# Turned query and key rows of a hybrid decoder layer: rounding and rest over 128 partitions, stored to DRAM by two transfers

## The chip, the cores and the metric

The kernel runs on one core of one Trainium2 chip. The metric is the time of one execution on the device in microseconds (us). A time taken with a profile comes with its span, from the first to the last instruction of the program on the core, and with the clock that the throttle granted to TensorE, as a share of full speed.

## The reference

One decoder layer over 1024 tokens of width 1024, in float32. One RMS norm and one input projection feed two head groups: differential attention (4 heads) and a gated delta rule (4 heads). Their outputs go through one output projection into the residual stream, and a squared-ReLU MLP of hidden width 4096 follows. What matters here is the differential attention:

```
da_q = rms_norm(da_q.reshape(B, S, DA_HEADS, 2, DA_QK_DIM), q_norm_w[l])
da_k = rms_norm(da_k.reshape(B, S, DA_HEADS, 2, DA_QK_DIM), k_norm_w[l])
...
s = jnp.einsum('bqhcd,bkhcd->bhcqk', qb, k, preferred_element_type=jnp.float32) * scale
...
a = p[:, :, 0] - lam * p[:, :, 1]
return jnp.einsum('bhqk,bkhe->bqhe', a.astype(v.dtype), v)
```

Each head has two softmax maps (index c) of 64 query and key channels each, so the channels of both maps fill 128 partitions.

## The kernel before

**Precision.** TensorE multiplies operands of a rounded type (fp32r in the profile). To keep float32 accuracy each operand is split into its rounded value and its rest (the value minus the rounded value), and products are summed over these parts. For the scores a matmul has room for 128 rows and a map has 64 channels, so for each map the rounded half and the rest are stacked in the partitions of one operand. With the query stacked the same way in `qa` and the other way round in `qb`, two matmuls against the stacked key `KS` (L1148, L1149) give all four products.

**Stages.** The first quarter of the span normalizes the input and computes the gated group's projections. Then comes a stage, from about 258 to 640 us, in which TensorE works through many streams at once: the scan of the gated group (`scan`, `scan_out`), the attention's input projections (`da_units`, `leave`), the turning of its queries and keys (`da_turns`), scores, values, the mixing transposes and the output projection. The rest of the span is the MLP.

**What sets the order.** In the middle stage a planner written into the kernel (`Interleave`) keeps an estimated TensorE time, `flow.now`, and estimated queues of the other engines. Each stream is a generator with a priority; it yields the time from which it can go on. `flow.chain` books instructions on the estimated queues and returns when their result should be there, with 180 ns for each change of engine and a margin of a quarter; `flow.hold` keeps a PSUM bank until then; `flow.put_off` puts a transfer's issue off until its estimated time. The order that comes out is fixed for TensorE. The other engines' orders come from the framework's scheduler. Transfers are issued on SP's queue, one after another, and an issue whose data is not there yet holds back what is behind it on that queue.

**Turning.** `leave` (L1028) takes a projection's PSUM bank `ps_qk` to SBUF on ScalarE (L1040) and normalizes it. `da_turns` (L957) then does 32 steps, one for each block of 128 tokens, for query or key, and for two pairs of heads: two transposes (L965, L966) put the 128 channels of two heads in the partitions of a PSUM tile, 256 columns (two heads of 128 tokens). For each map m, ScalarE rounds the map's 64 partitions into `qa[a, m, :]` (L972), and VectorE writes the rest, value minus rounded, to the other 64 partitions, `qa[b, m, :]` (L973). So a tile takes four instructions over 64 partitions, and `qa` holds each map's operand as it is used later. One transfer stores it (L977) to `qk_d`, where a partition's two maps and two heads lie in one run of 2 KB. `qa` has two buffers.

**Loading.** `load_head` (L1064) reads a head's keys of each map, rows of 512 bytes, and `load_q` (L1081) a block's queries: `qa` in one transfer, `qb` in two with the halves of the partitions exchanged. `load_unit` (L199) brings weights by the transfers of L211 into `wraw`, which ScalarE rounds (L213) and VectorE or GpSimd subtracts (L214). `scan` loads `pka` (L839), `scan_out` loads `pkb` and `zgt` (L894, L896) ahead of their use.

Of the kernel before, what the change touches and what calls it, by code (L numbers as in the profile page):

```python
# [9 lines left out]
F32 = mybir.dt.float32  # L10
F32R = mybir.dt.float32r
BF16 = mybir.dt.bfloat16
AF = mybir.ActivationFunctionType
ALU = mybir.AluOpType
# [4 lines left out]
P = 128  # L19
# [3 lines left out]
NT = SEQ // P  # L23
# [96 lines left out]
def act(n, accum=False):  # L120
    return "S", 55.0 + 0.83 * n + (93.0 if accum else 0.0)


def vec(n, extra=0.0):
    return "V", 68.0 + 1.045 * n + extra
# [7 lines left out]
def tile_hymba_layer(  # L133
# [6 lines left out]
    nc = tc.nc  # L140
    V, S, G, T = nc.vector, nc.scalar, nc.gpsimd, nc.tensor
# [9 lines left out]
    dram = ctx.enter_context(tc.tile_pool(name="dram", bufs=1, space=DRAM))  # L151
# [36 lines left out]
    fsg_d = dram.tile([P, 1024], F32, name="fsg_d")  # L188
    rt_d = dram.tile([SEQ], F32, name="rt_d")
    cgr_d = dram.tile([HEADS * SEQ], F32, name="cgr_d")  # L190
    qk_d = dram.tile([2, 2, NT, P, 2, 2, P], F32, name="qk_d")
    v_d = dram.tile([NT, P, 3, P], F32, name="v_d")
    acc_d = dram.tile([NT, P, DM], F32, name="acc_d")
    ud = {i: dram.tile([FF // 512, P, 2, 512], F32, name=f"ud{i}") for i in range(1, 8)}
# [261 lines left out]
    for tb in range(NT):  # L456
        T.matmul(tail[:, 300 + 2 * tb:302 + 2 * tb], ssum_[:, tb * P:(tb + 1) * P], ones[:, 0:2],
                 start=True, stop=True)
# [305 lines left out]
    flow = Interleave()  # L764
# [3 lines left out]
    HF = (slice(0, 64), slice(64, 128))  # L768
# [185 lines left out]

    late, accs, vts, v_at, qa_free = [], {}, {}, {}, [0.0] * 3

    def da_turns():  # L957
        for i in range(4 * NT):
            while not late:
                yield flow.now + 50, None  # L960
            g, kind, tb, qn, t = late[0]
            r = yield from flow.bank("px", at=max(t + 2000, qa_free[i % 2] - 500))
            late.pop(0)
            pt = px.tile([P, 512], F32, tag="px", name="ps_qkt")
            T.transpose(pt[:, 0:P], qn[:, 0:P], ident)  # L965
            T.transpose(pt[:, P:2 * P], qn[:, P:2 * P], ident)  # L966
            flow.begun(("qa", i % 2))
            qa = sd.tile([P, 2, 256], F32R, tag="qa", name="qa", bufs=2)
            wv = qw if kind == 0 else kw
            for m in range(2):  # L970
                a, b = HF[m], HF[1 - m]
                S.activation(qa[a, m, :], pt[a, 0:256], AF.Copy, scale=wv[a])  # L972
                V.scalar_tensor_tensor(qa[b, m, :], pt[a, 0:256], wv[a], qa[a, m, :].bitcast(F32),  # L973
                                       ALU.mult, ALU.subtract)
            flow.pe(2 * TR)
            t = flow.chain(act(256), act(256), vec(256, 60), vec(256, 60), start=max(flow.now, qa_free[i % 2]))
            flow.put_off(t, ("qa", i % 2), lambda g=g, kind=kind, tb=tb, qa=qa: nc.sync.dma_start(  # L977
                qk_d[g, kind, tb], qa.bitcast(F32).rearrange("p m (h t) -> p m h t", h=2)))
            qa_free[i % 2] = t + DMA_T
            flow.hold(r, t)  # L980
            state["turned"] += 1
            if state["turned"] % (2 * NT) == 0:
                flow.due(lambda t, key: key[0] == "qa")
                state["da"] += 1
                state["da_t"] = flow.now + 6000
        sdctx.close()
# [77 lines left out]
    def load_head(h, pool):  # L1064
        KS = []
        for m in range(2):
            k = pool.tile([P, SEQ], F32R, tag=f"KS{m}", name=f"KS{m}")
            nc.sync.dma_start(k.bitcast(F32).rearrange("p (b t) -> p b t", t=P),
                              qk_d[h // 2, 1, :, :, m, h % 2, :].rearrange("b p t -> p b t"))
            KS.append(k)  # L1070
        return KS

# [8 lines left out]
    def load_q(h, tb):  # L1081
        qa = ap.tile([P, 2, P], F32R, tag="qa", name="qa", bufs=2)
        qb = ap.tile([P, 2, P], F32R, tag="qb", name="qb", bufs=2)
        src = qk_d[h // 2, 0, tb, :, :, h % 2, :]
        nc.sync.dma_start(qa.bitcast(F32), src)
        nc.sync.dma_start(qb[HF[0]].bitcast(F32), src[HF[1]])
        nc.sync.dma_start(qb[HF[1]].bitcast(F32), src[HF[0]])
        return qa, qb
# [5 lines left out]
    def scores():  # L1094
        heads, loaded, npe, nsc, since = {}, {}, 0, 0, 0
        while state["da"] < 1:
            yield flow.now + 300, None
        heads[0] = load_head(0, ap), load_v(0, ap)
        q = load_q(*order[0])
        yield state["da_t"] + 3000, None  # L1100
        for u, (h, tb) in enumerate(order):
            if h == 1 and h not in heads:
                while not (state["scan"] and len(v_at) == NT):
                    yield flow.now + 300, None
                heads[1] = load_head(1, pools["a2"]), load_v(1, pools["a2"])
                loaded[1] = flow.now + 9000
            if h > 0 and state["da"] > 1 and 2 not in heads:
                heads[2] = load_head(2, ap), load_v(2, ap)
                loaded[2] = max(flow.now, state["da_t"]) + 4000
# [8 lines left out]
            if q is None and h > 0:  # L1118
                q = load_q(h, tb)
# [3 lines left out]
            if q is None:  # L1123
                q = load_q(h, tb)
                yield flow.now + 3000, None
# [381 lines left out]
    flow.add(2, values())  # L1507
    flow.add(3, scores())
    flow.add(1.6, da_turns())
    flow.add(4, da_units())  # L1510
    flow.add(1.4, mix_loads())
# [343 lines left out]
```

## Time and profile before

| | |
|---|---|
| median of 3 runs | 1226.64 us (1225.75 to 1227.22) |
| the profiled execution's own time | 1226.58 us |
| its span | 1224.9 us, at a mean granted clock of 0.998 |
| busy VectorE, ScalarE, GpSimd | 850.0, 604.6, 121.0 us |
| instructions of TensorE (matmuls) | 6330 |
| transfers `qk_d<-qa` | 32 of 256 KB, median 3.1 us from issue to landing |

The profiled execution's time is 1.7 us over its span; that part lies outside the program's instructions. It is 0.06 us under the median, so that sums made against it stand for the median too. A busy TensorE is not TensorE at its peak, since the ends of matmuls are modelled; what tells is whether it stood idle and what ended the wait. In the views by stretch, "DMA share" is the mean busy share of the core's 16 DMA engines.

### The profile page before, as it was taken

What the parts mean: (1) busy time and instruction counts of PE and PEld (TensorE: products, weight loads), DVE (VectorE), ACT (ScalarE), POOL (GpSimd) and SP (SyncE); (2) the same over time, 40 slices, a digit from 0 to 9 for tenths busy, and PEclk for the clock granted to TensorE, in tenths of its full rate; (3) what the DMA queues carried; (4) which work ended last, traced back from release to release, by engine and by line L of the source; (5) the groups of instructions that cost most, each with busy time, mean ns of one, the idle gap of its engine ahead of it and who ended that gap; (6) DMA issues with size and microseconds to landing.
All of it is one profiled execution on the core that took longest, in us unless ns stands there. A gap on an engine that the chain in (4) does not pass through costs nothing.

```text
span 1224.9 us, 17632 instructions
## 1 busy us (share of the span) xinstructions
PE 1212.0 (99%) x6330; PEld 1029.2 (84%) x6330; DVE 850.0 (69%) x1448; ACT 604.6 (49%) x1176; POOL 121.0 (10%) x162
## 2 busy tenths in 40 slices
PE   9999999999999999999999999999999999999998
PEld 9988888898888888888788888888888888888887
DVE  7786788477868577766798554566577955786553
ACT  8565545234556555656666444454554333333331
POOL 0011110223332230212100000000000000000000
PEclk9999999999999999999999999999999999999999
DMA  6564442456755584434528433443279855433301
GB/s 230 176 182 125 112 130 87 116 183 218 241 161 180 173 244 135 115 80 142 183 86 291 155 127 133 170 174 135 103 253 353 325 185 183 160 104 104 138 35 69
DMA packets 161087, 199.04 MB, mean 163 GB/s; under 512 B 21008, under 2 KB 120936, under 8 KB 161000
## 3 DMA queue, kind: packets, MB, share of 16 engines
q1 hardware_dynamic: 160856, 197.79, 49.3%
q8 instruction: 50, 0.82, 0.3%
q14 instruction: 37, 0.30, 0.1%
q10 hardware_dynamic: 144, 0.13, 0.0%
HBM read 132.32 MB, written 65.56 MB: 162 GB/s over the span
## 4 chain that ended last, share of the span: by engine, by line
PE 89%; DVE 4%; DMA 3%; ACT 2%; issue 1%; SPq 0%; POOL 0%; ACTq 0%; DVEq 0%
PE X L1454 5%; PE X L1453 5%; PE X L1452 5%; PE X L1768 4%; PE X L1769 4%; PE X L1770 4%; PE ps_dn L221 4%; PE ps_dn L219 4%; PE ps_dn L220 4%; PE ps_qk L1012 3%; PE Y L1454 3%; PE Y L1453 3%; PE Y L1452 3%; PE ps_qk L1014 3%; PE ps_qk L1013 2%; PE ps_o L1201 2%
## 5 line engine op out<-in xcount | busy, mean ns | idle before, releaser
L1371 ACT CAST hH<-ur 128x1024 fp32r<-128x1024 f32 x56 | 58.6, 1048 | 166.0 <-PE X L1769 79.7
L1372 DVE TENSOR_TENSOR hL<-ur,hH 128x1024 fp32r<-128x1024 f32 x56 | 68.5, 1224 | 79.8 <-ACT hH L1371 79.8
L1372 DVE TENSOR_TENSOR op<-raw,op 128x1024 fp32r<-128x1024 f32 x48 | 58.7, 1223 | 75.3 <-PE X L1453 42.3
L1768 PE MATMUL X<-hH 128*128 128x512 f32 x224 | 87.2, 389 | 0.0
L1769 PE MATMUL X<-hL,hH 128*128 128x512 f32 x224 | 87.2, 389 | 0.0
L1770 PE MATMUL X<-hH,hL 128*128 128x512 f32 x224 | 87.2, 389 | 0.0
L1012 PE MATMUL ps_qk<-wH,hH 128*128 128x512 f32 x192 | 82.2, 428 | 1.9 <-ACT qn L1040 1.9
L1014 PE MATMUL ps_qk<-wH,hL 128*128 128x512 f32 x192 | 75.8, 395 | 0.0
L219 PE MATMUL ps_dn<-hH,wH 128*128 128x512 f32 x192 | 75.7, 394 | 0.0
L220 PE MATMUL ps_dn<-hL,wH 128*128 128x512 f32 x192 | 75.6, 394 | 0.0
L1013 PE MATMUL ps_qk<-wL,hH 128*128 128x512 f32 x192 | 75.4, 393 | 0.1
L221 PE MATMUL ps_dn<-hH,wL 128*128 128x512 f32 x192 | 75.4, 393 | 0.0
L1372 DVE TENSOR_TENSOR hL<-dw,hH 128x1024 fp32r<-128x1024 f32 x56 | 68.2, 1220 | 3.2 <-ACT hH L1371 3.2
L1371 ACT CAST op<-raw 128x1024 fp32r<-128x1024 f32 x48 | 50.4, 1050 | 34.8 <-PE Y L1454 20.1
L1371 ACT CAST hH<-dw 128x1024 fp32r<-128x1024 f32 x56 | 58.6, 1047 | 16.7 <-DMA dw<-in_w_down_dram 5.1
L1157 ACT ACTIVATE pexp<-ps_sc,mx 128x128 f32<-128x128 f32 (+7 forms) x64 | 47.3, 740 | 26.1 <-DVE mx L1153 26.1
L595 DVE SCALAR_TENSOR_TENSOR cy<-cp,pv,cy 128x512 f32<-128x512 f32 x72 | 53.7, 750 | 7.8 <-ACT cy L593 7.0
L1153 DVE TENSOR_REDUCE mx<-ps_sc 128x1 f32<-128x128 f32 (+7 forms) x64 | 47.5, 754 | 14.1 <-PE ps_sc L1151 13.5
L1291 PE MATMUL ps_op<-wH,hH 128*128 128x512 f32 x128 | 53.6, 419 | 0.0
L1293 PE MATMUL ps_op<-wH,hL 128*128 128x512 f32 x128 | 50.3, 393 | 0.0
L1292 PE MATMUL ps_op<-wL,hH 128*128 128x512 f32 x128 | 50.0, 391 | 0.0
L1453 PE MATMUL Y<-hL,op 128*128 128x512 f32 x128 | 49.8, 389 | 0.0
(355 smaller groups left out, 3383.8 us busy)
## 6 DMA issues: line engine op xcount, KB each, us to landing
ur<-ud SPq DMA_DIRECT2D x28, 1024.0 KB, 4.9
raw<-in_w_up_dram SPq DMA_DIRECT2D x32, 512.0 KB, 3.7
dw<-in_w_down_dram SPq DMA_DIRECT2D x32, 512.0 KB, 7.2
qk_d<-qa SPq DMA_DIRECT2D x32, 256.0 KB, 3.1
ud<-ua SPq DMA_DIRECT2D x16, 512.0 KB, 4.0
ud<-s SPq DMA_DIRECT2D x16, 512.0 KB, 3.2
wraw<-in_w_in_dram SPq DMA_DIRECT2D x24, 256.0 KB, 3.5
wraw<-in_w_in_dram SPq DMA_DIRECT2D x48, 128.0 KB, 2.9
```

Of the source, the lines that this page charges most:

```text
L219: T.matmul(ps, lh(k), rh(k), start=(k == 0), stop=False)
L220: T.matmul(ps, lh(k), rl(k), start=False, stop=False)
L221: T.matmul(ps, ll(k), rh(k), start=False, stop=(k == n - 1))
L1012: T.matmul(ps, hH[:, 4 * kh + k, sl], wh[:, k, :], start=(kh + k == 0), stop=False)
L1013: T.matmul(ps, hH[:, 4 * kh + k, sl], wl[:, k, :], start=False, stop=False)
L1014: T.matmul(ps, hL[:, 4 * kh + k, sl], wh[:, k, :], start=False, stop=(kh + k == 4))
L1371: S.copy(dst[0], src)
L1372: V.tensor_tensor(dst[1], src, dst[0].bitcast(F32), ALU.subtract)
L1453: T.matmul(ps, op[0][:, k, cs], h[1][:, k, :], start=False, stop=False, skip_group_check=True)
L1768: T.matmul(o, v[0][:, j, sl], v[2][:, j, c], start=s0, stop=False, skip_group_check=True)
L1769: T.matmul(o, v[0][:, j, sl], v[3][:, j, c], start=False, stop=False, skip_group_check=True)
L1770: T.matmul(o, v[1][:, j, sl], v[2][:, j, c], start=False, stop=s1, skip_group_check=True)
```

## The change

The two maps are rounded together: one instruction of ScalarE over 128 partitions writes `qa[:, 0, :]` (rounded), one of VectorE writes `qa[:, 1, :]` (the rest). The halves no longer lie where the operands need them, so the store puts them there. `qk_d` is laid out with the map ahead of the partition, and two transfers store a tile: the rounded part to the first half of map 0 and the second half of map 1, which are blocks 0 and 3 of the four blocks of 64 rows; the rest to blocks 1 and 2. The planner's booking for a tile falls from two and two instructions to one and one. The loads read the same rows of 512 bytes from the new layout.

```diff
-    qk_d = dram.tile([2, 2, NT, P, 2, 2, P], F32, name="qk_d")
+    qk_d = dram.tile([2, 2, NT, 2, P, 2, P], F32, name="qk_d")
...
+    def store_halves(dst, qa):
+        blocks = dst.rearrange("m (j r) h t -> (m j) r (h t)", j=2)
+        for part, to in ((0, blocks[0:4:3]), (1, blocks[1:3])):
+            nc.sync.dma_start(to, qa[:, part, :].bitcast(F32))
+
...
-            for m in range(2):
-                a, b = HF[m], HF[1 - m]
-                S.activation(qa[a, m, :], pt[a, 0:256], AF.Copy, scale=wv[a])
-                V.scalar_tensor_tensor(qa[b, m, :], pt[a, 0:256], wv[a], qa[a, m, :].bitcast(F32),
-                                       ALU.mult, ALU.subtract)
+            S.activation(qa[:, 0, :], pt[:, 0:256], AF.Copy, scale=wv)
+            V.scalar_tensor_tensor(qa[:, 1, :], pt[:, 0:256], wv, qa[:, 0, :].bitcast(F32), ALU.mult, ALU.subtract)
             flow.pe(2 * TR)
-            t = flow.chain(act(256), act(256), vec(256, 60), vec(256, 60), start=max(flow.now, qa_free[i % 2]))
-            flow.put_off(t, ("qa", i % 2), lambda g=g, kind=kind, tb=tb, qa=qa: nc.sync.dma_start(
-                qk_d[g, kind, tb], qa.bitcast(F32).rearrange("p m (h t) -> p m h t", h=2)))
+            t = flow.chain(act(256), vec(256, 60), start=max(flow.now, qa_free[i % 2]))
+            flow.put_off(t, ("qa", i % 2), lambda g=g, kind=kind, tb=tb, qa=qa: store_halves(qk_d[g, kind, tb], qa))
...
-                              qk_d[h // 2, 1, :, :, m, h % 2, :].rearrange("b p t -> p b t"))
+                              qk_d[h // 2, 1, :, m, :, h % 2, :].rearrange("b p t -> p b t"))
...
-        src = qk_d[h // 2, 0, tb, :, :, h % 2, :]
+        src = qk_d[h // 2, 0, tb, :, :, h % 2, :].rearrange("m p t -> p m t")
```

## The prediction

> **What bounds the kernel now.** The page comes first: which engine has no slack, and what the DMA engines carry.
>
> ```profile
> PE 1212.0 (99%) x6330; PEld 1029.2 (84%) x6330; DVE 850.0 (69%) x1448; ACT 604.6 (49%) x1176; POOL 121.0 (10%) x162
> ...
> DMA  6564442456755584434528433443279855433301
> GB/s 230 176 182 125 112 130 87 116 183 218 241 161 180 173 244 135 115 80 142 183 86 291 155 127 133 170 174 135 103 253 353 325 185 183 160 104 104 138 35 69
> ```
>
> TensorE (PE) is the bound. Its work stays, in amount and kind, so the change can take away only what PE waits, or add waits. A DMA digit of 9 (slice 31, 353 GB/s) shows what 16 busy engines move: 22 GB/s each, 46 ns for 1 KB.
>
> Next the stretches in which the touched line L972 runs, with clock and DMA share of the whole core:
>
> ```profile
> core 0: us, ACT busy (x), PEclk, DMA share, GB/s
> 258.00:300.00 42.00, 9.08 (x20) 1.00 0.69 216
> 300.00:340.00 40.00, 7.08 (x16) 0.96 0.72 230
> 340.00:380.00 40.00, 3.74 (x8) 1.00 0.56 168
> 380.00:420.00 40.00, 4.21 (x9) 1.00 0.65 194
> 420.00:460.00 40.00, 5.16 (x11) 1.00 0.72 217
> 460.00:500.00 40.00, 0.00 (x0) 1.00 0.41 121
> ```
>
> With two such instructions for a tile, 10, 8, 4, 4.5 and 5.5 tiles are turned and stored in the five stretches, 18 of them in the first 82 us. There the DMA engines are already 0.7 busy. Then the waits of 258 to 460 us (us in total, times, longest):
>
> ```profile
> ACT qa L972 <- DVE qa L973: 15.1, 16, 1.8
> ...
> ACT wH L213 <- DMA wraw<-in_w_in_dram: 9.6, 5, 4.9
> ...
> ACT qa L972 <- DMA qk_d<-qa: 2.8, 1, 2.8
> ...
> PE ps_qk L1012 <- ACT qn L1040: 1.9, 1, 1.9
> ```
>
> PE's longest wait in this stage is the last one. The timeline shows how it arises on ScalarE (ACT):
>
> ```profile
> 297.99 1.96 SPq L211 DMA_DIRECT2D wraw<-in_w_in_dram  x4
> 303.87 1.34 ACT L213 CAST wH<-wraw 128x512 fp32r<-128x512 f32 x2 [4.86 <-DMA wraw<-in_w_in_dram]
> 306.81 0.47 ACT L972 ACTIVATE qa<-ps_qkt,pv 64x256 fp32r<-64x256 f32 x1 [0.87 <-DVE qa L973]
> 308.05 0.69 ACT L1040 ACTIVATE qn<-ps_qk,rt 128x512 f32<-128x512 f32 x1
> ```
>
> ACT works in order. It stood 4.86 us for a weight transfer, then again for VectorE, and so emptied PE's bank late. Late transfers therefore reach PE directly here.
>
> **The change part by part.** The four instructions of a tile:
>
> ```profile
> L973 DVE SCALAR_TENSOR_TENSOR qa<-ps_qkt,pv,qa 64x256 fp32r<-64x256 f32 x32 | 15.4, 483 | 7.5 <-ACT qa L972 6.6
> L973 DVE SCALAR_TENSOR_TENSOR qa<-ps_qkt,qw,qa 64x256 fp32r<-64x256 f32 x32 | 15.4, 482 | 6.1 <-ACT qa L972 5.4
> L972 ACT ACTIVATE qa<-ps_qkt,pv 64x256 fp32r<-64x256 f32 x32 | 15.0, 468 | 24.1 <-PE ps_qkt L966 12.9 <-DVE qa L973 7.6 <-DMA qk_d<-qa 2.8
> L972 ACT ACTIVATE qa<-ps_qkt,qw 64x256 fp32r<-64x256 f32 x32 | 14.9, 466 | 10.9 <-DVE qa L973 7.5 <-PE ps_qkt L966 3.2
> ```
>
> *Compute.* 32 instructions go on each engine. What one over 128 partitions costs is not in the trace at 256 columns, but its neighbours are:
>
> ```profile
> L856 DVE SCALAR_TENSOR_TENSOR sr<-ps_A,neg_eg,pka 128x128 f32<-128x128 f32 x24 | 6.8, 344 | 0.3 <-PE ps_A L852 0.2
> L1035 ACT ACTIVATE qn<-ps_qk,rt 128x384 f32<-128x384 f32 x8 | 4.6, 577 | 0.0
> L260 DVE SCALAR_TENSOR_TENSOR hL<-ps_tr,mw,hH 128x512 fp32r<-128x512 f32 x4 | 3.0, 747 | 0.8 <-ACT hH L259 0.7
> L1034 ACT ACTIVATE vt<-ps_qk,rt 128x128 f32<-128x128 f32 x8 | 2.9, 363 | 4.4 <-PE ps_qk L1014 4.4
> ```
>
> Halfway between 363 and 577 is 470 ns; a third of the way from 344 to 747 is 478 ns. So partitions cost nothing, and ACT sheds 32 x 0.467 = 14.9 us, VectorE 32 x 0.482 = 15.4 us. The tile's chain loses its two middle steps, and with them ACT's waits for VectorE (15.1 us over 16 times). All of this lies beside PE's work, except in PE's 1.9 us wait. The planner books 0.83 us less for a tile (one ACT and one VectorE instruction with their margin), the chain itself loses 0.47 + 0.48 = 0.95 us, so the plan's slack does not shrink. It does shift PE's order, which I price at -2 to +2 us, the longest wait of the stage, and take as 0.
>
> *SP.* 32 issues are added. Their price is between the old store and a transfer of the same count of rows in two runs:
>
> ```profile
> L977 SPq DMA_DIRECT2D qk_d<-qa x32: 319/327/778, 264.6 to 455.7; - x32
> L1086 SPq DMA_DIRECT2D qb<-qk_d x32: 517/562/2037, 270.4 to 558.9; - x32
> SPq L977 <- DVE qa L973: 17.7, 16, 4.0
> ```
>
> That is 10.5 to 18 us of SP in 202 us. Behind them wait weights (L211) and the scan's loads (L839, L894). The second store waits for VectorE as the one store did (17.7 us), but for one instruction, not two; both ends about cancel, 0.
>
> *The transfers.* This is where I see the price. The bytes stay. The 2 KB rows become 1 KB rows:
>
> ```profile
> q1 hardware_dynamic: 41214, 41.20, 66.4%
> ...
> qk_d<-qa SPq DMA_DIRECT2D x32, 256.0 KB, 3.1
> ...
> KS<-qk_d SPq DMA_DIRECT2D x6, 512.0 KB, 5.3
> ...
> pkb<-park_d SPq DMA_DIRECT2D x23, 128.0 KB, 3.9
> ```
>
> In 258 to 460 us 41,214 packets of 1.0 KB on average took 0.664 x 16 x 202 us, so 52 ns each; 46 ns by the busiest slice. Dealt evenly, a half-store puts 8 rows on each of 16 engines, 0.4 us: no change. But the rounded half goes to blocks 0 and 3. These two blocks of 64 rows cannot be told as one run of 128, as the old store could and as blocks 1 and 2 can, which touch. The transfer's outermost count is then 2. If the engines are dealt by that count, two engines carry 64 rows each: 64 x 52 ns = 3.3 us, or 2.9 us at 46 ns. The views do not print how a transfer is dealt. I take dealing by blocks: in the trace's raw semaphore updates, which no view prints, short transfers tell their landing in as many parts as they have outermost rows, the 128-row store in sixteen. Only the choice hangs on this, no price.
>
> The Trainium skill, "DMA: Bandwidth & Descriptors", section "Why a DMA increments its semaphore by 16 and not by 1", says it as a rule: the engine count is the largest number up to 16 that divides both sides' slowest dimension, on the lowest-numbered engines. By that rule it is two engines, always the same two; by even dealing the sum would be rival one's. No run here shows it yet for a store of this size.
>
> On these two engines a tile then costs 3.3 + 0.4 us, less the old 8 rows of 2 KB (0.8): +2.9 us; at 46 ns +2.6. Their load by stretch, share x length + tiles x 2.9: 29 + 29 = 58 of 42 us (+16); 29 + 23 = 52 of 40 (+12); then 34 of 40, 39 of 40, 45 of 40. At 340 us they are 28 us behind. With 46 ns and the bytes over 353 GB/s in place of the shares, 26 + 26 = 52 of 42 and 26 + 21 = 47 of 40: 17 us behind. Every other transfer has a sixteenth of its rows on each, and is as late. How late may it be?
>
> ```profile
> 261.98 1.74 SPq L894 DMA_DIRECT2D pkb<-park_d  x4
> ...
> 270.32 0.94 PE L905 MATMUL ps_o<-S,pkb 128*128 128x128 f32 x7
> ```
>
> The scan's loads, issued by 263.7 and landing in 3.9 us, have some 3 us to spare; weights have none (4.86 us above), nor has the second `qa` buffer (2.8 us). So PE, whose order is fixed, takes 17 - 3 = 14 to 28 - 3 = 25 us. I take 17.5, nearer the lower end, since a busy stage's packet times hold waits for each other. After 340 us the load fits, and at 0.41 from 460 us it drains.
>
> Sum: 1226.6 + 17.5 + 0 + 0 = **1244 us**. It is made against the profiled 1226.58 us, which stands for the median of 1226.64.
>
> **The rivals.** *One, faster: even dealing.* Then ACT's queue ahead of L1040 at 308.05 loses an instruction and the 0.87 us wait, the weights' issue at 297.99 comes up to 0.5 us sooner, and PE's wait of 1.9 us shrinks to none. With it goes a clock drop:
>
> ```profile
> 306.00:310.00 4.00, 2.09 (x9) 1.36 (x9) 3.81 (x9) 2.89 (x8) 1.71 (x2) 0.96 0.59 164
> 310.00:314.00 4.00, 4.00 (x19) 3.64 (x18) 3.90 (x10) 2.73 (x8) 2.23 (x3) 0.62 0.65 205
> ```
>
> (PE, its loads, VectorE, ACT, GpSimd, clock, DMA.) At 0.96 and 0.62, 4 x 0.04 + 4 x 0.38 = 1.7 us of clock are lost. Together 3.6 us: **1223 us**. It decides if the store's engines are sixteen. "TensorE: Matmul & The Clock Gate" of the Trainium skill, section "What's actually happening", has the clock fall after an idle window of about 3.4 us. The wait here was 1.9 us and the clock fell; the measurement decides. By the rule the drop would not be this wait's, and the gain 1.9 us.
>
> *Two, no change.* Dealing is even, and the wait at 306 us stays because the weight transfer's landing sets it; or the backlog hides. **1226 us**. Against the second: weights have no slack.
>
> *Three, much slower.* Blocks 1 and 2 are not joined either. Both halves lie on two engines: 6.7 - 0.8 = 5.8 us for a tile, 32 x 5.8 = 187 us on top of 0.664 x 202 = 134, in 202 us: some 120 us more, **1345 us**.
>
> **How the numbers follow.** The forecast has 0.78, rival one 0.10, rival two 0.08, rival three 0.04. What this kernel's measurement can tell from no change is about 0.2%, 2.5 us. Of the forecast's case, 0.04 may still end within that and 0.01 below. Slower is 0.73 + 0.04 + 0.04 from shifted order in the other cases = 0.81; the same 0.04 + 0.06 = 0.10; faster 0.09. The range reaches down to rival two, 1226, and up to the late loads' 25 us with six more clock drops of 1.7 us, 1262. Left out are rivals one and three and the tails. The forecast's own range is 1236 to 1262.
>
> **What would show it.** Right: the first store's landing at 5 us or more beside some 3 for the second; pka, pkb and wraw landing several us later in 270 to 340 us; ACT's waits for DMA far over 9.6 us and PE's after 300 us over 10 us in total; the DMA share lower, though transfers are late. L972 and L973 at 32 instructions of some 470 and 480 ns in any case. Wrong: equal landings of both stores and unchanged loads.

## The result and the profile after

The changed kernel takes 1261.22 us (median of 5 runs, 1259.23 to 1263.36) against 1226.74 (5 runs, 1225.75 to 1227.22): 2.8% slower, ratio 1.0283 [1.0268, 1.0298]. The profiled execution took 1259.23 us with a span of 1257.5, 32.6 us more than the 1224.9 of before. The prediction was 1244 us (1226 to 1262), slower: the direction and the place are right, the amount is half.

The page after, beside the rows of before:

```profile
PE 1223.0 (97%) x6330; PEld 1037.3 (82%) x6330; DVE 828.3 (66%) x1416; ACT 589.3 (47%) x1144; POOL 122.2 (10%) x162
...
DMA  6654433456655657333355545343368955422311
```

TensorE's busy time rose from 1212.0 to 1223.0 us with the same 6330 matmuls: 11.0 us of slower clock (the mean granted clock fell from 0.998 to 0.990). Its idle time, span less busy, rose from 12.9 to 34.5 us: 21.6 us of waiting. Together they are the 32.6 us. VectorE and ScalarE have less to do (850.0 to 828.3, 604.6 to 589.3), and that bought nothing.

The stretches in which tiles are turned show where both were lost (TensorE's busy time, granted clock, DMA share):

```profile
core 0: us, PE busy (x), PEclk, DMA share, GB/s
258.00:300.00 42.00, 36.14 (x219) 0.96 0.62 171
300.00:340.00 40.00, 35.58 (x193) 0.96 0.68 190
340.00:380.00 40.00, 32.60 (x174) 0.91 0.59 163
380.00:420.00 40.00, 36.29 (x204) 0.98 0.50 143
420.00:460.00 40.00, 38.43 (x205) 0.98 0.63 173
460.00:500.00 40.00, 35.96 (x176) 0.91 0.73 213
```

The same stretches of the kernel before:

```profile
258.00:300.00 42.00, 41.89 (x281) 1.00 0.69 216
300.00:340.00 40.00, 37.99 (x218) 0.96 0.72 230
340.00:380.00 40.00, 39.05 (x219) 1.00 0.56 168
...
460.00:500.00 40.00, 39.52 (x245) 1.00 0.41 121
```

In the six stretches TensorE stood 27.0 us, against 5.1 before. The DMA share fell in the first two, although transfers are late: most engines stand still more. And the loss does not end at 340 us. The waits from 258 to 500 us show where it arises (us in total, times, longest):

```profile
ACT qa L975 <- DMA qk_d<-qa: 28.5, 7, 6.8
ACT wH L213 <- DMA wraw<-in_w_in_dram: 17.3, 7, 4.6
...
PE ps_sc L1149 <- DMA KS<-qk_d: 6.3, 1, 6.3
...
PE ps_qk L1013 <- ACT qn L1041: 4.0, 1, 4.0
```

The first row was 2.8 us, once, before: ScalarE wants to write the next tile and finds the buffer still being stored. The second was 9.6 us. TensorE's own waits end in several ways. From 258 to 640 us they come to 29.0 us: 11.7 are ended by a transfer itself (loads of the stored keys and queries, `pkb`, and `mt` for the mixing transposes), 9.9 by ScalarE, 7.4 by VectorE. Before they were 7.1 us, 0.2 of them ended by a transfer.

The chain of waits of the same stretch passes through these stores; these are its pieces that the transfer `qk_d<-qa` ended (start, length in us), of which the 75 longest pieces of before's chain there hold none:

```profile
263.45 7.44 DMA qk_d<-qa
285.25 7.63 DMA qk_d<-qa
...
294.70 7.32 DMA qk_d<-qa
302.62 7.18 DMA qk_d<-qa
...
341.37 6.97 DMA qk_d<-qa
```

SP issues the stores of two tiles together:

```profile
261.64 2.42 SPq L960 DMA_DIRECT2D qk_d<-qa  x4
```

Some 7.3 us each time is what the two tiles' first stores take, one after the other, at the predicted 3.3 us, and 0.7 for the rest. The trace's raw semaphore updates, which no view prints, bear it out. They tell a landing in parts: two for a first store (after one update some 1 us from its issue), sixteen for a second. Of these four stores the two first ones were complete 4.9 and 7.7 us after their issue. Of the second ones' sixteen parts fourteen came within 3.1 and 5.0 us, the last two only after 4.5 and 7.4 us. So a transfer on sixteen engines is complete only when the two busy engines have done their share of it.

What follows the second piece stands in the timelines of ScalarE and TensorE:

```profile
289.77 0.47 ACT L975 ACTIVATE qa<-ps_qkt,pv 128x256 fp32r<-128x256 f32 x1 [6.52 <-DMA qk_d<-qa]
293.40 0.47 ACT L975 ACTIVATE qa<-ps_qkt,qw 128x256 fp32r<-128x256 f32 x1 [3.15 <-DMA qk_d<-qa]
293.77 0.68 ACT L1041 ACTIVATE qn<-ps_qk,rt 128x512 f32<-128x512 f32 x1
294.50 0.50 PE L1013 MATMUL ps_qk<-wH,hH 128*128 128x512 f32 x1 [4.01 <-ACT qn L1041]
```

ScalarE stands 6.52 and 3.15 us, L1041, which empties TensorE's bank, comes behind, and TensorE waits 4.01 us for it. After the first piece TensorE waits for a late transfer instead. From 268 to 272 us the DMA engines do this:

```profile
268.00:272.00 4.00, 2.80 (x16) 1.00 0.14 42
```

0.14 of sixteen engines is 2.2 engines: the first stores are being finished. TensorE lost 1.2 of these 4 us to a load of the scan, issued by 265.6 us:

```profile
271.27 0.84 PE L905 MATMUL ps_o<-S,pkb 128*128 128x128 f32 x4 [1.20 <-DMA pkb<-park_d]
```

The touched instructions are as predicted, 16 of each form:

```profile
L976 DVE SCALAR_TENSOR_TENSOR qa<-ps_qkt,pv,qa 128x256 fp32r<-128x256 f32 x16 | 7.7, 480 | 20.1 <-ACT qa L975 16.7 <-DMA zgt<-zg_d 3.4
L975 ACT ACTIVATE qa<-ps_qkt,qw 128x256 fp32r<-128x256 f32 x16 | 7.5, 471 | 23.4 <-DMA qk_d<-qa 9.9 <-PE ps_qkt L971 9.2 <-DMA acc<-in_x_dram 4.3
```

### The profile page after: what moved, and what is told of

Read it like the earlier page. It is cut to its first block, busy times and chain, and to the rows that moved or that the text cites. A ratio compares the mean times of both kernels' runs of the same rounds, so it can differ in the third digit from the quotient of the medians.

```text
span 1257.5 us, 17635 instructions
## 1 busy us (share of the span) xinstructions
PE 1223.0 (97%) x6330; PEld 1037.3 (82%) x6330; DVE 828.3 (66%) x1416; ACT 589.3 (47%) x1144; POOL 122.2 (10%) x162
## 4 chain that ended last, share of the span: by engine, by line
PE 87%; DMA 7%; DVE 2%; issue 2%; ACT 1%; SPq 1%; POOL 0%; ACTq 0%; DVEq 0%; POOLq 0%
PE X L1455 5%; PE X L1454 5%; PE X L1453 5%; PE X L1769 4%; PE X L1770 4%; PE X L1771 4%; PE ps_dn L219 3%; PE ps_dn L220 3%; PE ps_dn L221 3%; DMA qk_d<-qa 3%; PE Y L1455 2%; PE Y L1454 2%; PE Y L1453 2%; PE ps_qk L1013 2%; PE Z L1769 2%; PE Z L1770 2%
## 5 line engine op out<-in xcount | busy, mean ns | idle before, releaser
L1373 DVE TENSOR_TENSOR op<-raw,op 128x1024 fp32r<-128x1024 f32 x48 | 58.7, 1223 | 74.8 <-PE X L1454 34.5
L213 ACT CAST wH<-wraw 128x512 fp32r<-128x512 f32 x64 | 37.1, 624 | 36.2 <-DMA wraw<-in_w_in_dram 22.3
```

The costliest lines, as they stand in the source:

```text
L1373: V.tensor_tensor(dst[1], src, dst[0].bitcast(F32), ALU.subtract)
```

## Experiments

Losses and gains are against the kernel before, run on the same chip in the same series (medians 1225.1 to 1225.3 us).

### Is it the first store's shape?

**The same work, dealt evenly.** `three` keeps the change and stores the rounded part by two transfers of one block each:

```diff
-        for part, to in ((0, blocks[0:4:3]), (1, blocks[1:3])):
-            nc.sync.dma_start(to, qa[:, part, :].bitcast(F32))
+        for part, rows, to in ((0, HF[0], blocks[0]), (0, HF[1], blocks[3]), (1, slice(0, P), blocks[1:3])):
+            nc.sync.dma_start(to, qa[rows, part, :].bitcast(F32))
```

> The changed kernel, but the rounded part goes out by two transfers of one block of 64 rows each, so three transfers for a tile; the outermost count of each is a multiple of 16. Theory (the two blocks of the first store put 64 rows on each of two DMA engines, and everything behind them is late): the loss goes, about 1222 to 1229 us, landings of the stores about 3 us, ACT's waits for stores under 6 us. Rival (the loss comes of the added issues on SP and of the planner's new order): 32 more issues make it no faster than the changed kernel, 1258 us or more.

Measured: 1230.65 us, ratio 1.0044 [1.003, 1.0057]. `inter` puts rounded and rest of a partition in neighbouring rows of DRAM, so that both transfers go to 128 rows at a constant stride (the loads take every second row instead of a half):

```diff
-        for part, to in ((0, blocks[0:4:3]), (1, blocks[1:3])):
-            nc.sync.dma_start(to, qa[:, part, :].bitcast(F32))
+        rows = dst.rearrange("m q h t -> (m q) (h t)")
+        for part in range(2):
+            nc.sync.dma_start(rows[part::2], qa[:, part, :].bitcast(F32))
```

> The changed kernel with the rounded and the rest row of a channel side by side in DRAM: row 2p holds the rounded row of partition p, row 2p+1 its rest. Both stores are then 128 rows at one stride, the loads of qa and of the keys one run of 128 rows, and qb is loaded as before by two transfers, of every second row. The operands' partitions are in another order, the same for queries and keys. Two transfers for a tile as in the changed kernel. Theory (dealing by the outermost count): the loss goes with the same number of issues, 1220 to 1228 us; with the waits of TensorE near 306 us gone too, 1223. Rival (issues, 1 KB rows and order): 1255 us or more.

Measured: 1227.13 us, ratio 1.0018 [1.001, 1.0027]. Either way most of the 34 us is gone.

**The store alone, in the kernel before.** `before_spare2` leaves the kernel before as it is and adds an unused store of 128 KB per tile to blocks 0 and 3 of a spare tensor; `before_spare16` writes blocks 1 and 2 (`1:3`), otherwise the same:

```diff
+    spare_d = dram.tile([4 * NT, 4, 64, 256], F32, name="spare_d")
...
+        nc.sync.dma_start(spare_d[state["spare"], 0:4:3], qa[:, 0, :].bitcast(F32))
```

> The kernel before with one more store for a tile, of its first 128 rows of 1 KB, to a part of DRAM that nothing reads, in blocks 0 and 3 of four. Computation, plan and order are those of before. Theory: two DMA engines get 64 x 46 to 52 ns = 2.9 to 3.3 us more for each of 32 tiles; as in the changed kernel, TensorE waits longer, 1245 to 1275 us. Rival (order and planner): only the 32 issues are added, 1226 to 1230 us.

> The same spare store, to blocks 1 and 2 of four, which touch and are one run of 128 rows. Theory: 8 rows on each of 16 engines, 0.4 us, some 13 us of each engine's 202 us: 1226 to 1231 us. Rival (any added store of this size and count costs it, by SP's issues or by the bytes): like the other spare store, over 1240 us.

Measured: 1259.62 us, 1.0279 [1.0264, 1.0295], and 1225.64 us, 1.0004 [0.9995, 1.0013]. The page's row of the first, with a span of 1258.5 us, and its wait for the buffer:

```profile
PE 1223.3 (97%) x6330; PEld 1035.6 (82%) x6330; DVE 847.5 (67%) x1448; ACT 604.9 (48%) x1176; POOL 120.5 (10%) x162
```

```profile
ACT qa L978 <- DMA qk_d<-qa: 25.1, 8, 7.8
```

The same bytes, the same issue, the same buffer; only the place of the two blocks differs, and with it 34 us: 35.2 us idle and a busy time of 1223.3, as in the changed kernel. That the first store's destination makes the loss is shown. Here TensorE's longest wait, 4.91 us, is for VectorE, behind late weights:

```profile
319.09 1.35 ACT L214 CAST wH<-wraw 128x512 fp32r<-128x512 f32 x2 [6.22 <-DMA wraw<-in_w_in_dram]
319.74 0.69 DVE L215 TENSOR_TENSOR wL<-wraw,wH 128x512 fp32r<-128x512 f32 x1 [4.93 <-ACT wH L214]
320.75 2.07 PE L865 MATMUL ps_A<-sr,lt 128*128 128x128 f32 x8 [4.91 <-DVE sr L857]
```

### How does the loss grow?

The prediction let a backlog add up over stretches. By that reckoning a store on more engines, or every second store, fits and costs little. `spare4` and `spare8` cut the spare tensor into 8 and 16 blocks and write every second one; `spare2_small` writes half the rows on two engines; `spare2_alt` issues the two-engine store after every second tile:

```diff
+    spare_d = dram.tile([4 * NT, 8, 32, 256], F32, name="spare_d")
+        nc.sync.dma_start(spare_d[state["spare"], 0:8:2], qa[:, 0, :].bitcast(F32))
...
+    spare_d = dram.tile([4 * NT, 4, 32, 256], F32, name="spare_d")
+        nc.sync.dma_start(spare_d[state["spare"], 0:4:3], qa[HF[0], 0, :].bitcast(F32))
...
+        if state["spare"] % 2 == 0:
+            nc.sync.dma_start(spare_d[state["spare"], 0:4:3], qa[:, 0, :].bitcast(F32))
```

> The kernel before, and after each tile's store a second, unused store of 128 KB whose outermost count in DRAM is 4 instead of 2 (1.7 us on each of four engines by 52 ns a row, in place of 3.3 us on two). Backlog theory: the loss is what these engines cannot carry; 29 + 17 = 46 of 42 us and 29 + 13 = 42 of 40, so about 6 us behind, 3 of them covered: 1228 to 1231 us. Rival, a fixed price for each narrow store in proportion to the time on its engines: half of the 33 us that two engines cost, 1243 us. Rival, the loss is in the number of transfers: 1260 us.

> The same spare store over 8 engines (0.8 us on each). Backlog theory: 29 + 8 = 37 of 42 us fits, no loss, 1226 us. Proportional price: a quarter of 33 us, 1235 us.

> The kernel before, and after each tile's store an unused store of 64 KB on two engines (32 rows of 1 KB on each, 1.65 us). If the time on the slowest engine sets the loss, whatever the number of engines and bytes: as with four engines and 128 KB, 1234.5 us. If bytes or the number of engines set it: 1230 us (half the bytes) or 1250 to 1260 us (two engines as before).

> The kernel before, and the unused two-engine store of 128 KB after every second tile's store only: 16 of them, on average 1.65 us of two engines for a tile, but 3.3 us at a time. If the loss follows the mean load of a stretch, as with four engines (1.65 us for every tile, 1234.5): 1232 to 1237 us. If each narrow store has a price by its own length, half of the 33 us: 1242 us. If the clock only drops in long waits, and those need two narrow stores close together: below half, 1232 to 1238 us and a clock of 1.0.

| kernel | stores x time on an engine (at 52 ns a row) | time, us | ratio | loss per store, us |
|---|---|---|---|---|
| `before_spare2` | 32 x 3.3 | 1259.62 | 1.0279 [1.0264, 1.0295] | 34.4 / 32 = 1.08 |
| `spare2_alt` | 16 x 3.3 | 1240.97 | 1.0127 [1.0113, 1.014] | 15.8 / 16 = 0.99 |
| `spare4` | 32 x 1.65 | 1234.54 | 1.0083 [1.0068, 1.0097] | 9.3 / 32 = 0.29 |
| `spare2_small` | 32 x 1.65 | 1235.75 | 1.008 [1.0064, 1.0095] | 10.6 / 32 = 0.33 |
| `spare8` | 32 x 0.8 | 1229.74 | 1.0033 [1.002, 1.0046] | 4.5 / 32 = 0.14 |
| `before_spare16` | 32 x 0.4 | 1225.64 | 1.0004 [0.9995, 1.0013] | 0.5 / 32 = 0.01 |

By the raw semaphore updates the unused store lands in 2, 4, 8 or 16 parts, as the time on an engine in the table supposes. The medians from issue to landing are 6.2 us in `before_spare2`, 5.5 in `spare2_alt`, 4.5 in `spare4`, 4.3 in `spare2_small`, 3.3 in `spare8` and 2.9 in `before_spare16`.

Two readings. `spare4` and `spare2_small` differ in bytes and in the number of engines and agree in the loss: the time on the slowest engine sets it. And each store has its own price: half as many cost nearly half, though on average they load the two engines no more than `spare4` loads its four. The backlog theory falls: it had some 2 to 6 us for `spare4`, none for `spare8`. So does the price in proportion to the length: a store twice as long costs some three times as much (0.33 to 1.08).

`half` asks the same of the changed kernel: keys by three transfers, queries by the change's two.

```diff
+        three = ((0, HF[0], blocks[0]), (0, HF[1], blocks[3]), (1, slice(0, P), blocks[1:3]))
+        two = ((0, slice(0, P), blocks[0:4:3]), (1, slice(0, P), blocks[1:3]))
+        for part, rows, to in three if kind else two:
```

> The changed kernel with its rounded part stored by two transfers of one block each on 16 engines (as in the kernel with three transfers, 1230.7) for the key tiles, and by the change's two-engine transfer for the query tiles alone: 16 narrow stores of 32. Same loss for each narrow store: half way between 1230.7 and 1261.2, 1246 us. Loss by load and by clock drops, so below half: 1235 to 1241 us.

Measured: 1243.39 us, 1.0154 [1.0137, 1.017]. That is 12.7 us over `three` for 16 narrow stores, 0.80 each, where the changed kernel is 30.6 us over it for 32, 0.96 each. It lies nearer the half way of 1246 us than the 1235 to 1241 of the other forecast, but the price is not quite the same.

Why the mean load misleads can be read in the kernel before, microsecond by microsecond (the last two columns are DMA share and GB/s):

```profile
266.00:267.00 1.00, 1.00 (x9) 0.83 (x8) 0.92 (x4) 0.40 (x3) 0.10 (x1) 1.00 0.73 274
267.00:268.00 1.00, 1.00 (x9) 0.94 (x8) 0.54 (x2) 0.49 (x2) 1.00 (x2) 1.00 0.12 43
268.00:269.00 1.00, 1.00 (x6) 0.79 (x5) 1.00 (x5) 0.95 (x3) 1.00 (x1) 1.00 0.00 0
269.00:270.00 1.00, 1.00 (x6) 0.84 (x5) 1.00 (x5) 0.44 (x1) 0.93 (x2) 1.00 0.65 186
270.00:271.00 1.00, 1.00 (x10) 0.92 (x9) 0.97 (x2) 0.00 (x0) 0.40 (x1) 1.00 1.01 314
```

A share of 0.69 over 42 us is made of bursts at 1.0 and pauses at 0. A pause is no reserve for what stands in a burst, or for what waits for one tile's store.

### Does it matter where, and in which queue?

`spare2_late` issues the 32 two-engine stores behind the first 32 stores of the MLP's sums, from 654 us on, where TensorE waits for nothing:

```diff
             for d, t in puts.pop(0):
                 nc.sync.dma_start(d, t)
+                if state["spare"] < 4 * NT:
+                    nc.sync.dma_start(spare_d[state["spare"], 0:4:3], t[:, 0, 0:256])
```

> The kernel before, and the 32 unused two-engine stores (128 KB each) not beside the turned tiles but behind the first 32 stores of the MLP's sums, about 700 to 900 us, where the DMA share is 0.40: 80 + 32 x 3.3 = 186 of 200 us, and PE waits for nothing. Backlog theory: 1226 to 1230 us, the later figure if single transfers of that stage come late. Fixed price of a two-engine store: 1260 us here too.

Measured: 1226.23 us, 1.0005 [0.9996, 1.0014]. The same 32 stores cost nothing there: there is no price of a two-engine store as such. They even landed later, at a median of 9.8 us by the raw updates, and ScalarE waited 20.5 us for their buffers; TensorE did not wait for ScalarE.

What stays open after this is the path: the tile's own buffer, or the other transfers behind the store. `spare2_free` stores the constant identity, so that no buffer hangs on it:

```diff
-        nc.sync.dma_start(spare_d[state["spare"], 0:4:3], qa[:, 0, :].bitcast(F32))
+        nc.sync.dma_start(spare_d[state["spare"], 0:4:3].rearrange("j r (a t) -> j r a t", a=2),
+                          ident.unsqueeze(1).broadcast_to([P, 2, P]))
```

> The kernel before, and after each tile's store an unused two-engine store of 128 KB that reads a constant (the identity, twice a row, in packets of 512 bytes) instead of the tile, so that no buffer hangs on it. If the loss comes from the tile's two buffers, which ScalarE finds occupied (28.5 us of its waits in the changed kernel, 25.1 with the spare store from the tile): 1226 to 1235 us. If it comes from the other transfers behind it on the two engines: the same 1255 to 1262 us.

Measured: 1302.7 us, 1.0631 [1.0615, 1.0647]. It does not answer the question: a store that depends on no tile was issued early by the framework's scheduler, all 32 between 26.6 and 130.6 us. But it shows the store by itself. SP's timeline, the stretches (TensorE's busy time, clock, DMA share, GB/s) and the longest wait for a transfer there:

```profile
26.58 48.10 SPq L960 DMA_DIRECT2D spare_d<-ident  x17
```

```profile
40.00:50.00 10.00, 3.38 (x29) 0.86 0.14 43
50.00:60.00 10.00, 0.00 (x0) 0.50 0.14 43
60.00:70.00 10.00, 0.00 (x0) 0.50 0.14 43
```

```profile
ACT wH L214 <- DMA wraw<-in_w_in_dram: 49.5, 1, 49.5
```

Seventeen stores took SP 48.1 us, 2.8 us each, while only about two of sixteen engines moved anything; ScalarE waited 49.5 us for a weight transfer and TensorE stood. That SP's later issues wait behind narrow stores is shown here; in the stage of the change SP is not held up like that, an issue of the unused store takes 0.5 us in `before_spare2`.

`spare2_actq` and `after_actq` issue the narrow store from ScalarE's queue:

```diff
-        nc.sync.dma_start(spare_d[state["spare"], 0:4:3], qa[:, 0, :].bitcast(F32))
+        nc.scalar.dma_start(spare_d[state["spare"], 0:4:3], qa[:, 0, :].bitcast(F32))
...
+        for part, to, eng in ((0, blocks[0:4:3], nc.scalar), (1, blocks[1:3], nc.sync)):
+            eng.dma_start(to, qa[:, part, :].bitcast(F32))
```

> The kernel with the unused two-engine store from the tile (1259.6), this store issued by ScalarE on its own queue instead of SyncE's. If transfers wait behind it because they stand in the same queue: 1226 to 1240 us. If the two engines' time is what counts, whatever the queue: 1250 to 1262 us.

> The changed kernel, the rounded part's two-engine store issued by ScalarE. Queue order: 1228 to 1242 us. Engine time: 1252 to 1264 us. The buffer still waits for the narrow store itself in both.

Measured: 1265.53 us, 1.0327 [1.0312, 1.0343], and 1275.63 us, 1.0413 [1.0395, 1.0431]. Issued from another queue the store costs more, not less. The waits of `spare2_actq` from 258 to 500 us:

```profile
ACT qa L978 <- DMA qk_d<-qa: 17.9, 4, 8.4
...
ACT qa L978 <- DMA spare_d<-qa: 7.2, 3, 3.8
```

17.9 + 7.2 = 25.1 us for the buffer, just what it was in SP's queue. In the changed kernel's version the same wait is 38.7 us, against 28.5. Part of the difference between the queues may be ScalarE's 32 issues; no run separates that.

### What is the relief of ScalarE and VectorE worth?

`inter_oldplan` is `inter` with the planner's old booking, `inter1` is `inter` with one store of 128 rows of 2 KB, as before:

```diff
-            t = flow.chain(act(256), vec(256, 60), start=max(flow.now, qa_free[i % 2]))
+            t = flow.chain(act(256), act(256), vec(256, 60), vec(256, 60), start=max(flow.now, qa_free[i % 2]))
...
-        for part in range(2):
-            nc.sync.dma_start(rows[part::2], qa[:, part, :].bitcast(F32))
+        nc.sync.dma_start(rows.rearrange("(p a) x -> p (a x)", a=2), qa.bitcast(F32).rearrange("p a x -> p (a x)"))
```

> Both stores on sixteen engines (rounded and rest in alternate rows of DRAM), the change's two instructions per tile, but the planner books the old four. If the plan's new order is what ate the 3.6 us of rival one: faster than before, 1223 to 1225 us. If the relief of ScalarE and VectorE is worth nothing whatever the order: 1226 to 1227 us, as with the new booking (1227.1).

> The change's two instructions over 128 partitions, rounded and rest of a partition in neighbouring rows of DRAM, so that one transfer of 128 rows of 2 KB stores both, as in the kernel before: no added issue, no narrow store. If the 32 added issues cost something, below the 1227.1 of the kernel with two such transfers and, with rival one's 3.6 us, down to 1223 us. If nothing is left to gain beside PE: 1225 to 1227 us, the same as before.

Measured: 1227.55 us, 1.0013 [1.0004, 1.0021], and 1225.25 us, 0.9998 [0.9989, 1.0007]. The old booking gains nothing: its interval overlaps that of `inter`. With the change's instructions and the old number of transfers the time is that of before, with 32 transfers more it is 0.18% above (`inter`), with 64 more (`three`) 0.44%: intervals that do not meet, some 2.5 us for 32. But `inter_oldplan` has the 32 too, and its interval meets that of `inter1`; and `before_spare16` also added 32 and lost nothing. So whether the added transfers cost, and by which of their parts, is open. No version beats the kernel before.

## Why the prediction was right in direction and short in size

**The mechanism held.** The first store was predicted to lie on two engines, 3.3 us of each, and to make weights and the second `qa` buffer late. 0.14 of sixteen engines in `spare2_free` and in the changed kernel, the pieces of 7.3 us in the chain, 28.5 and 17.3 us of ScalarE's waits (2.8 and 9.6 before), the landings in two parts, and the pair `before_spare2` and `before_spare16` bear it out. The rule cited from the Trainium skill, "DMA: Bandwidth & Descriptors", section "Why a DMA increments its semaphore by 16 and not by 1", agrees with the number of parts in which the stores of these runs land (2, 4, 8 or 16). Which engines they are no run shows.

**The step that failed is the size of the transfers' term,** in three places. First, "I take 17.5, nearer the lower end": TensorE waited 21.6 us more, in the upper half of the 14 to 25. Second, clock drops stood only in the range and at zero in the sum; they are 11.0 us, near the 6 x 1.7 us of the range's top. 21.6 + 11.0 is the whole growth of the span, 32.6 us for a term of 17.5. Third, the reckoning behind the term, "At 340 us they are 28 us behind" and "After 340 us the load fits", is not what happens: TensorE lost 7.4 us from 340 to 380 and 4.0 from 460 to 500 (40 less the busy time; 1.0 and 0.5 before), and the runs with fewer, shorter or wider stores lose more than their mean load allows. The prediction's own 45 of 40 us for 420 to 460 does not fit either. In its place the runs show a price for each two-engine store of 128 KB, 0.8 to 1.1 us of the kernel's time, as long as something hangs on its landing. That the pieces of the chain stay near 7 us, and do not grow, speaks for TensorE's waiting stretching the stage, so that nothing adds up over tiles; that is a reading, not tested.

**The ways to TensorE are read, not isolated.** The traces show three: the buffer, ScalarE's queue and TensorE's bank (4.01 us at 294.50); loads of what was stored, the keys above all (6.3 us); and other late transfers (`pkb`, and the weights of `before_spare2`). The sum had the buffer and the late transfers, and did not name the loads. SP itself stood 19.8 us for landings of `qk_d` from 258 to 500 us (5.0 before), with all that was behind it on its queue. How the loss divides among them stays open: no run gave the tiles a third buffer. Nor does any run tell the planner of the slower landing. It counts a buffer as free 2.5 us after its store (`DMA_T`); the changed kernel's first stores take 4.8 us and more.

**Compute.** L975 and L976 take 470 and 480 ns at 128 partitions, as interpolated; 32 instructions less are 15.3 us less on ScalarE. VectorE shed 21.7 us, more than the 15.4 of L973; where the rest lies is open. All of it was hidden, as predicted.

**The plan's order and SP** were taken at 0. The booking is worth nothing (`inter_oldplan`). The added transfers are worth up to some 2.5 us (`inter` against `inter1`) or nothing (`before_spare16`), where the sum had nothing.

**The rivals.** Rival one needed even dealing, and `inter1` is that case: it took the time of before (1225.25 us against 1225.13), not 3.6 us less. Those 3.6 us were one execution's wait and clock drop, and where they go others come: `inter1`'s longest wait of TensorE from 258 to 640 us is 1.7 us for `qa`. Rival three falls with the lone loss of 34 us.

**The signs.** The landings that the prediction named are not printed for the changed kernel; the raw semaphore updates give them, from 258 to 340 us. The first store took 4.9 to 7.8 us, as forecast. The second, forecast at some 3, took 6.8 at the median: its last two parts stand behind the first store. `pka` came later, at a median of 6.0 us against 3.9 before, but of its sixteen parts the fourteenth came after 3.7 us, against 3.6. `pkb` came later only at its longest (7.1 us against 4.6), and the weights not at the median (3.6 against 3.7); why ScalarE waits longer for them there is open.

## What to carry to other kernels

A DRAM destination made of separate blocks can cost far more than its bytes: write it as rows at a constant stride (`inter`) or split the store at the blocks (`three`), and look for a DMA share near 2 of 16 while something waits. Size such a transfer by its own length against the waits that hang on it (its buffer, the loads of what it stores, the other transfers on its engines), not by mean load, and add the clock that long waits take. Relief on engines that are not the bound was worth nothing here (`inter1`): ask first which wait of the bound engine it would end.

## What the runs showed of the hardware

The price of a store is steep in its length: 0.01, 0.14, 0.3 and 1.0 us of the kernel's time for 0.4, 0.8, 1.65 and 3.3 us on its engines (at 52 ns a row), in this stage; and nothing in a stage in which TensorE does not wait.

A transfer to sixteen engines is complete with its slowest part: behind two-engine stores fourteen parts of the second store came in 3.1 us and the last two in 4.5.

SP's issue itself was slow with seventeen such stores in a row: 2.8 us each in `spare2_free`, beside a median of some 0.5 in `before_spare2` and `spare2_late`.

The clock does not follow one wait's length. Before, a wait of 1.91 us preceded a drop to 0.62 in the slice from 310 to 314 us; `spare4` waited 3.00 us near the same place, and the clock did not drop:

```profile
309.56 1.16 PE L865 MATMUL ps_A<-sr,lt 128*128 128x128 f32 x8 [3.00 <-DVE sr L857]
```

```profile
304.00:308.00 4.00, 2.56 (x18) 1.00 0.77 229
308.00:312.00 4.00, 2.44 (x15) 1.00 0.84 263
312.00:316.00 4.00, 4.00 (x22) 1.00 0.59 160
```

What else decides is open. In the changed kernel a drop follows the wait of 4.01 us shown above (busy time, clock):

```profile
292.00:296.00 4.00, 1.39 (x5) 0.96 0.52 162
296.00:300.00 4.00, 4.00 (x23) 0.61 0.69 197
```
